# Linear attention moved between the delta-rule scan and softmax attention, with projections as its filler, and new bank and load rules

## The chip, the cores and the metric

One core of one Trainium2 chip runs the kernel. The metric is the device time in microseconds of one execution. The kernel before ran three times: 2265.18, 2269.78 and 2278.88 us, median 2269.78 us.

## The reference

Two layers of a diffusion backbone over 512 latent tokens `x` and 256 context tokens, model width 1024, float32. One layer, cut to what matters here:

```python
p = split(rmsnorm_and_modulate(h) @ w_in)          # one input projection, all head groups
# 1. multi-head latent attention (MLA), 8 heads
q, k, v = rmsnorm(cq) @ w_uq, rmsnorm(ckv) @ w_ukv  # ranks 384 and 256; rope on 32 columns
mla = softmax(q @ k.T * scale) @ v                  # latents see context + latents
# 2. gated delta rule (GDN), 4 heads, two directions, chunks of 64
v_new = u - w @ S
o = qd @ S + A @ v_new
S = S * g_last + k_end.T @ v_new                    # one step per chunk, strictly in order
# 3. gated linear attention (GLA), 4 heads, two directions
o = q_t S_t ; S_t = diag(exp(la_t)) S_(t-1) + k_t.T v_t
# all three: head norm, gate with silu(z), then one output projection
h = h + gate * rmsnorm(concat(mla, gdn, gla) @ w_out)
h = h + gate * rmsnorm(conv_ffn(...))
```

The last layer gives latents only, so its context queries, and the delta rule's outputs on context chunks, are left out.

## The kernel before, in words

All activations are held transposed, features on partitions and 768 tokens (context 0 to 255, latents 256 to 767) along the free axis. A projection by float32 weights is made of three products of split halves: `wsplit` (L196) loads a raw tile `wr` (three buffers), ACT casts its high half `wh` (L191) and DVE subtracts the low half `wl` (L192); `fprod` and its generator form `fsteps` then issue high*low, low*high and high*high matmuls over the column segments (512 latents, 256 context) into `bb`, a pair of PSUM banks (two such pairs). The other four banks have the names a, b, c and d; `ab(tags)` hands them out in turn, from the string it is given or from `self.tags`.

The order within one layer (`layer`, L311):

1. `project_in` computes the parts of the input projection that the delta rule needs, with `gdn_prep` and `gdn_tile` (products of 32x32 blocks for the inverse of each chunk pair, six tiles of two chunks) beside it. What the delta rule does not need is a generator `rest`: `gla_kq`, `gla_v`, `mla_in` and, last, `gate(1)`, the silu gates of the linear attention. At its end `project_in` runs the scan with `rest` as `self.fill`; `pace(n)` takes n steps of the generator, one step being a few matmuls.
2. `gdn_scan` (L969): 12 steps, both directions in one instruction stream, state `Sb`. A step multiplies state by key and query (16 matmuls of 128 columns, `ks`), makes `r = v - ks*eg` (L996, L997), multiplies by the inverse (`vp`, 16 matmuls), scales it (`vs`, L1008), multiplies by the keys (`up`, 16 matmuls) and adds it to the state (L1022, after POOL has multiplied the state by its decay, L1018). The output (`tq`, L1026, product with `AT`, L1041) and `head_out` (L1065: square, reduce, reciprocal root, POOL multiply L1075, two transposes, gate L1082) stand in the same step. `pace(8)` is called twice in a step. All its PSUM tiles rotate over b and c; the filler has a and d.
3. `mla_project` (L1250): products with `w_uk`, `w_uq`, `w_uv`; results that attention needs go to DRAM (`Kd`, `Qd`) and come back.
4. `attention` for the first pair of heads (`EP`, 1 of 4), then `gla`, then attention for the other three pairs with banks a and b. Per head and tile of 128 queries: scores into `bb`, row maximum (L1377), exponential into `P` (L1380), transposes of `P` (L215) copied out by ACT (L1394) or DVE (L1392), products with `V` into `a` or `b`.
5. `w_out` (k order 4, 5, 6, 7, 0, 1, 2, 3: delta rule and linear attention first), `post`, `prenorm`, feed-forward network.

The program text is not the final order. A list scheduler places each instruction on its engine by readiness in its own time model, with program order as the priority, so instructions of a later stage run ahead where their data and buffers allow it: attention is placed beside scan and linear attention alike. Pools bound this: a pool that takes the place of a closed one waits for the last reader of the old one. All DMAs are issued by SP, in one queue that keeps its order: a store that waits for its data (`ungates`, L1064) holds every load placed behind it.

Of the kernel before, what the change touches and what calls it, by code (L numbers as in the profile page):

```python
# [11 lines left out]
F32 = mybir.dt.float32  # L12
# [29 lines left out]
SN = (8, 8)  # L42
# [3 lines left out]
EP = (1, 1)  # L46
WO = ((4, 5, 6, 7, 0, 1, 2, 3), (4, 5, 6, 7, 0, 1, 2, 3))
SPF = 0
# [3 lines left out]
HB = 14  # L52
# [83 lines left out]
class Net:  # L136
# [40 lines left out]
    def s1(self, pool=None):  # L177
        return (pool or self.B).tile([128, 256], F32, name=self.nm("s"), tag="s", bufs=4 if pool is None else 6)
# [17 lines left out]

    def wsplit(self, src, n=1024):

        raw = self.raw()
        self.nc.sync.dma_start(raw[:, :n], src)  # L200
        his, los = [], []
        for o in range(0, n, 512):
            w = min(512, n - o)
            hi = self.W.tile([128, 512], F32R, name=self.nm("wh"), tag="wh", bufs=WB)
            lo = self.W.tile([128, 512], F32R, name=self.nm("wl"), tag="wl", bufs=WB)
            self.split(raw[:, o:o + w], hi[:, :w], lo[:, :w], self.nc.gpsimd if (o // 512, self.ph) in WP else None)
            his.append(hi)
            los.append(lo)
        return his, los
# [101 lines left out]
    def layer(self, l, later):  # L311
# [25 lines left out]
        Ap, self.A = self.pool("A")  # L337
        A0p, self.A0 = self.pool("A0")
        A1p, A1 = self.pool("A1")
        with self.ahead(HM):  # L340
            self.mla_project(A1)
# [7 lines left out]
        self.close(Bp)  # L349
        self.Xp, X = self.pool("X", "right")  # L350
# [10 lines left out]
        self.tags = "ab"  # L361
# [104 lines left out]
    def ada(self, l, mods, raw=None):  # L466
# [4 lines left out]
        for m in mods:  # L471
            for h in range(4):
                raws = []
                for k in range(2):
                    rt = (raw or self.raw)()
                    nc.sync.dma_start(rt, self.a["w_ada"][l, 4 * m + h, k])
# [76 lines left out]
    def project_in(self, later):  # L553
# [62 lines left out]
        def gdn(m):  # L616
            dst = dsts[m]
            for i in range(2):
# [3 lines left out]
                for a, b in segs:  # L622
# [7 lines left out]
                    if m != 1:  # L630
                        sq = self.F2.tile([128, 512], F32, name=self.nm("sq"), tag="sq", bufs=2)
# [7 lines left out]
        self.cq, self.ckv = [], []  # L639
        self.rr = self.small(12, "rr", 2)  # L640
# [48 lines left out]
        def projections():  # L689
# [29 lines left out]
        self.fill = [rest]  # L719
        self.tags = "ad"  # L720
        self.gdn_scan()
        self.fill = []
        drain(rest)
# [246 lines left out]
    def gdn_scan(self):  # L970
# [9 lines left out]

        for n in range(12):
# [24 lines left out]
            self.pace(SN[1])  # L1006
            vs = s1()
            nc.vector.tensor_tensor(vs.rearrange(h4, h=4), vp[:, :256].rearrange(h4, h=4),  # L1008
                                    self.eks[:, n].unsqueeze(2).to_broadcast(b4), op=ALU.mult)
            for d in range(2):  # L1010
                t, hf = ch[d] // 2, ch[d] % 2
                up = self.ab("bc")
# [10 lines left out]
            if need_o:  # L1023
                m = (3 if n < 4 else 15) - n
                vn, tq = s1(), s1()
                nc.vector.tensor_tensor(tq.rearrange(h4, h=4), ks[:, 256:].rearrange(h4, h=4), eg, op=ALU.mult)  # L1026
                if m < n:
                    nc.gpsimd.tensor_tensor(tq, tq, ost[m], op=ALU.add)
                nc.scalar.copy(vn, vp[:, :256])
                op = self.ab("bc")  # L1030
                for h in range(4):
                    for d in range(2):
                        e = d * 4 + h
                        self.mm(op[half[d], h * 64:(h + 1) * 64], self.AT[ch[d] // 2][half[d], e * 64:(e + 1) * 64],
                                vn[half[d], h * 64:(h + 1) * 64], True, True)
                if m > n:
                    ost[n] = self.C.tile([128, 256], F32, name=self.nm("ost"), tag="ost", bufs=4)
                    nc.vector.tensor_tensor(ost[n], tq, op[:, :256], op=ALU.add)
                    continue

                nc.vector.tensor_tensor(tq, tq, op[:, :256], op=ALU.add)  # L1041
                if n % 2 == 0:
                    lo = min(n, m) - 1
                    pieces = [(lo * 64, lo * 64 + 256)] if n < 10 else [(256, 384), (640, 768)]
                    zt = self.gates(0, pieces)
                first = (4 if n >= 10 else lo) if n % 2 == 0 else first
# [20 lines left out]
    def head_out(self, o, zt, cols, i):  # L1067
# [8 lines left out]
        ps = self.ab("cd" if i else "bc")  # L1076
# [8 lines left out]
    def gla(self):  # L1085
# [11 lines left out]
        for a, b in (CS, XS):  # L1097
# [34 lines left out]
            for d in range(2):  # L1132
# [22 lines left out]
                for st in steps:  # L1155
# [21 lines left out]
            def two():  # L1177
                t = self.B.tile([128, 1024], F32, name=self.nm("q2"), tag="q2", bufs=3)
                return t[:, :2 * n].rearrange("p (y c) -> p y c", y=2)
# [6 lines left out]
            for li, w in enumerate((32, 16, 8, 4, 2, 1, 0)):  # L1186
# [21 lines left out]
                for x in range(2):  # L1208
# [3 lines left out]
                    for i in range(nt):  # L1212
                        for c in range(2):
# [3 lines left out]
                                              ps[:, :nt * 128].rearrange("p (e j) -> p e j", j=64))  # L1217

            for i in range(nt):
                t, sl = t0 + i, slice(i * 128, (i + 1) * 128)  # L1220
                pieces = [(a + i // 2 * 256, a + i // 2 * 256 + 256)]
                if i % 2 == 0:
                    zt = self.gates(1, pieces)
# [22 lines left out]
                self.head_out(o, zt, [p0, p0 + 64], 1)  # L1246
                if i % 2:
# [3 lines left out]
    def mla_project(self, A1):  # L1251
# [12 lines left out]
        for lst, hi, lo, x in ((self.ckv, kvh, kvl, 0), (self.cq, cqh, cql, o)):  # L1264
            for d, h_, l_ in zip(lst, hi, lo):
                f = self.raw()
                nc.sync.dma_start(f[:, x:T], d[:, x:])
# [22 lines left out]
        for e in range(2):  # L1290
            rope = at("tab", 1)
            nc.sync.dma_start(rope, self.a["rope"][e])
            for p in range(4):
                wh, wl = self.wsplit(self.a["w_uq"][l, 2 * p + e], 384)
                ps = self.bb()
                self.fprod(ps, wh, wl, cqh, cql, self.osegs, 3)
# [10 lines left out]
        for t in range(6):  # L1307
# [8 lines left out]
            self.V.append(v)  # L1316

    def pair(self, pool, p):
# [8 lines left out]
        def raw(d, o):  # L1327
            f = self.raw()
            nc.sync.dma_start(f[:, o:T], d[:, o:])
# [236 lines left out]
```

## Time and profile before

| | |
|---|---|
| three timed runs | 2265.18 to 2278.88 us, median 2269.78 us |
| profiled execution | 2278.35 us |
| its span on the core | 2276.6 us |
| PE busy in the span | 2045.0 us, 90% |
| DVE, ACT, POOL busy | 1310.4, 1008.7, 536.0 us |
| mean granted TensorE clock | 0.934 of full speed |
| instructions | 44601 |

Time outside the span is 1.75 us, so a change of the span is a change of the time. The profiled execution lies 0.4% above the median. Columns of times are in microseconds, means in nanoseconds. A clock of 1.00 is 2.4 GHz and 0.50 is 1.2 GHz; values between are means over a stretch at both levels.

### The profile page before, as it was taken

To read this page: it belongs to the slowest core of one execution; us is meant where nothing else is said; L and a number is where in the kernel's file an instruction comes from. 1 tells how busy PE (TensorE), PEld (TensorE's weight loads), DVE (VectorE), ACT (ScalarE), POOL (GpSimd) and SP (SyncE) were. 2 spreads that over 40 slices of the span, in tenths; PEclk is the share of its full clock that TensorE was granted. 3 is DMA by queue.
4 is the path that set the end of the run, shared out by engine and by line. 5 is a ranking of instruction groups with operands and counts; after the bars stand their busy time and mean duration, and the time that the engine had idled before them with its cause. 6 is when DMAs were issued, how large, how long until landed. Compare 5 with 4: busy or idle time off the path is not lost. (4 is left out here: it accounts for less than half of the span.)

```text
span 2276.6 us, 44601 instructions
## 1 busy us (share of the span) xinstructions
PE 2045.0 (90%) x18168; PEld 1672.8 (73%) x18168; DVE 1310.4 (58%) x2474; ACT 1008.7 (44%) x1928; POOL 536.0 (24%) x897
## 2 busy tenths in 40 slices
PE   7898999888888799999999969988988777999996
PEld 4677777765667578888888857876766567888886
DVE  3354535668845743354454686556667757655556
ACT  4553323565464633332232456633446446543333
POOL 1342121135502310000010143413122613211102
PEclk8799999998898999999999979999989988999997
DMA  6232345422042354422212333111412053323322
GB/s 262 67 118 100 109 148 164 143 66 68 13 149 92 121 179 167 157 103 65 66 57 66 102 109 124 61 44 62 155 43 96 6 171 102 111 94 96 99 94 92
DMA packets 85134, 235.64 MB, mean 104 GB/s; under 512 B 9088, under 2 KB 24896, under 8 KB 84928
## 3 DMA queue, kind: packets, MB, share of 16 engines
q1 hardware_dynamic: 84928, 232.78, 30.7%
q8 instruction: 143, 2.34, 0.4%
q14 instruction: 63, 0.52, 0.1%
HBM read 204.04 MB, written 28.70 MB: 102 GB/s over the span
## 5 line engine op out<-in xcount | busy, mean ns | idle before, releaser
L212 PE MATMUL bb<-hh,wl 128*128 128x512 f32 (+1 forms) x1520 | 548.3, 361 | 18.0 <-DVE wl L192 10.9
L212 PE MATMUL bb<-hl,wh 128*128 128x512 f32 (+1 forms) x1520 | 542.0, 357 | 5.8 <-POOL hl L550 4.4
L192 DVE TENSOR_TENSOR wl<-wr,wh 128x512 fp32r<-128x512 f32 (+2 forms) x452 | 338.3, 751 | 362.3 <-ACT wh L191 361.0
L212 PE MATMUL bb<-hh,wh 128*128 128x512 f32 (+1 forms) x1520 | 540.2, 355 | 0.0
L191 ACT CAST wh<-wr 128x512 fp32r<-128x512 f32 (+2 forms) x452 | 274.1, 611 | 518.0 <-PE bb L212 370.3
L212 PEld LDWEIGHTS bb<-hh,wl 128*128 128x128 f32 x1520 | 293.2, 193 | 75.2 <-DVE wl L192 14.0
L212 PEld LDWEIGHTS bb<-hl,wh 128*128 128x128 f32 x1520 | 292.8, 193 | 49.4 <-POOL hl L550 7.8
L212 PEld LDWEIGHTS bb<-hh,wh 128*128 128x128 f32 x1520 | 292.9, 193 | 39.6 <-issue 2.1
L212 PE MATMUL bb<-g,wh 128*128 128x512 f32 (+1 forms) x1024 | 263.7, 349 | 2.3 <-DVE g L192 2.3
L1441 POOL TENSOR_SCALAR y<-u,fmt 128x512 f32<-128x512 f32 (+2 forms) x88 | 80.6, 917 | 527.1 <-ACT u L824 525.6
L212 PEld LDWEIGHTS bb<-g,wh 128*128 128x128 f32 x1024 | 181.5, 195 | 27.5 <-DVE g L192 3.3
L212 PE MATMUL bb<-g,wl 128*128 128x512 f32 (+1 forms) x512 | 180.3, 354 | 21.4 <-DVE wl L192 8.5
L212 PEld LDWEIGHTS bb<-g,wl 128*128 128x128 f32 x512 | 99.2, 195 | 36.9 <-ACT g L191 9.3
L824 ACT ACTIVATE u<-bb,fmt 128x512 f32<-128x512 f32 (+1 forms) x118 | 69.0, 613 | 85.0 <-PE bb L212 85.0
L212 PE MATMUL bb<-mh,wl 128*128 128x256 f32 (+1 forms) x256 | 85.2, 333 | 23.4 <-DVE wl L192 15.5
L1468 DVE TENSOR_TENSOR y<-y,bb 128x512 f32<-128x512 f32 (+2 forms) x80 | 54.8, 686 | 82.3 <-PE bb L212 82.2
L505 POOL TENSOR_TENSOR acc<-acc,sq 128x256 f32<-128x256 f32 (+1 forms) x48 | 49.5, 1031 | 183.9 <-ACT sq L503 180.9
L1442 DVE SCALAR_TENSOR_TENSOR y<-u,fmt,y 128x512 f32<-128x512 f32 (+2 forms) x88 | 72.3, 822 | 29.6 <-POOL y L1441 29.6
L212 PE MATMUL bb<-ml,wh 128*128 128x256 f32 (+1 forms) x256 | 84.1, 329 | 0.3
L1380 ACT ACTIVATE P<-bb,ast,srq 128x768 f32<-128x768 f32 (+1 forms) x80 | 72.6, 908 | 23.4 <-DVE ast L1378 14.5
L212 PE MATMUL bb<-mh,wh 128*128 128x256 f32 (+1 forms) x256 | 82.9, 324 | 0.0
L1377 DVE TENSOR_REDUCE ast<-bb 128x1 f32<-128x768 f32 (+1 forms) x80 | 67.2, 842 | 15.9 <-PE bb L212 15.6
(519 smaller groups left out, 3680.4 us busy)
## 6 DMA issues: line engine op xcount, KB each, us to landing
wr<-in_ffn_w_in SPq DMA_DIRECT2D x92, 512.0 KB, 3.5
wr<-in_w_ada SPq DMA_DIRECT2D x80, 512.0 KB, 3.9
wr<-in_ffn_w_out SPq DMA_DIRECT2D x48, 512.0 KB, 3.5
wr<-in_w_in SPq DMA_DIRECT2D x40, 512.0 KB, 4.3
wr<-in_w_out SPq DMA_DIRECT2D x32, 512.0 KB, 3.5
aw<-in_w_ada SPq DMA_DIRECT2D x16, 512.0 KB, 8.5
x<-in_xT SPq DMA_DIRECT2D x16, 384.0 KB, 8.7
wr<-in_w_uq SPq DMA_DIRECT2D x16, 192.0 KB, 2.6
```

What stands on the lines that cost most here:

```text
L191: self.nc.scalar.copy(hi, src)
L192: (eng or self.nc.vector).tensor_tensor(lo, src, hi.bitcast(F32), op=ALU.subtract)
L212: self.nc.tensor.matmul(out, l, r, start=start, stop=stop)
L505: (nc.vector, nc.gpsimd)[k % 2].tensor_tensor(acc[k % 2], acc[k % 2], sq, op=ALU.add)
L824: nc.scalar.activation(u[:, a + o:b + o], ps[:, off + a:off + b], AF.Identity, bias=bias)
L1377: nc.vector.reduce_max(st[:, 0:1], sc, axis=AX)
L1380: nc.scalar.activation(P[:, :w], sc, AF.Exp, bias=st[:, 0:1], scale=self.srq[:, t:t + 1], accum_out=st[:, 1:2])
L1441: nc.gpsimd.tensor_scalar(yv, u[:, lo + 1:lo + 1 + n], cw[1], self.fm(P_FCB + i), op0=ALU.mult, op1=ALU.add)
L1442: nc.vector.scalar_tensor_tensor(yv, u[:, lo:lo + n], cw[0], yv, op0=ALU.mult, op1=ALU.add)
L1468: nc.vector.tensor_tensor(y, y, p, op=ALU.add)
```

## The change

- Scan out of `project_in`: `project_in` returns `rest`, and the scan runs after it. The scan's pool C is now opened after F0 is closed; `sq` of the preparation moves from pool F2 to G.
- `gdn_scan` rewritten: fixed banks (`ks` and first half of `up` in b, `vp` and second half in c, both output products in d, `head_out` in a); the output products follow the state update; `head_out` and the store (`ungates`) of a step are put behind the next step's state update (`late`); `pace(5)` once per step.
- `gate(1)` moves ahead of `mla_in` in `rest`.
- `gla` runs between scan and attention, with a generator `beside` as filler: the remainder of `rest`, then `mla_project` (now a generator). `until` waits for the parts that `gla` needs; `pace` is called with `GN`.
- Attention follows: two pairs of heads before the mixed tiles are loaded, two behind; the last attention has banks a to d in place of a and b.
- `load`: the loads of weights and of `mla_project`'s and attention's operands are issued under a scheduler priority of 600 places.
- Buffers: `h` 14 to 12, `q2` 3 to 2, the scan's `s` 6 to 8.

```diff
-SN = (8, 8)
+SN = 5
-EP = (1, 1)
+EP = (2, 2)
+GN = (8, 6, 5)
+LP = 600
-HB = 14
+HB = 12
...
+    def load(self, out, src):
+
+        with self.tc.high_priority(offset=LP):
+            self.nc.sync.dma_start(out, src)
+
     def wsplit(self, src, n=1024):
 
         raw = self.raw()
-        self.nc.sync.dma_start(raw[:, :n], src)
+        self.load(raw[:, :n], src)
...
+    def until(self, what):
+
+        while what not in self.have:
+            self.pace(1)
...
+        F1p, F1 = self.pool("F1", "right")
         Fp, self.F = self.pool("F", "right")
+
+        F0p, self.F1 = self.pool("F0", "right")
+        rest = self.project_in(later)
+        self.close(F0p)
+        self.F1 = F1
         Cp, self.C = self.pool("C", "right")
-        F1p, self.F1 = self.pool("F1", "right")
-        F2p, self.F2 = self.pool("F2", "right")
-        self.project_in(later)
-        for p in (self.Hp, F2p, F1p, Cp, Fp):
+        self.fill = [rest]
+        self.gdn_scan()
+        for p in (Cp, Fp):
             self.close(p)
+
         Bp, self.B = self.pool("B", "right")
...
+        def beside():
+            yield from rest
...
+            yield from self.mla_project(self.A1)
+
+        self.tags = "ab"
+        self.fill = [beside()]
+        self.until("gla")
+        self.gla()
+        for g in self.fill:
+            drain(g)
...
-        with self.ahead(HA):
-            self.attention(A2, range(EP[l]))
-        with self.ahead(HG):
-            self.gla()
+        self.attention(A2, range(EP[l]))
...
-        self.tags = "ab"
+        self.tags = "abcd"
         self.attention(A2, range(EP[l], 4), mh, ml, mixed)
...
             yield from gla_v()
+            self.have.add("gla")
+            yield from gate(1)
+            self.have.add("gate")
             yield from mla_in(0)
             if not last:
                 yield from mla_in(1)
-            yield from gate(1)
...
-            ks = self.ab("bc")
-            for y in range(2 if need_o else 1):
-                for d in range(2):
-                    c = ch[d]
-                    for x in range(2):
-                        self.mm(ks[half[d], y * 256 + x * 128:y * 256 + x * 128 + 128],
-                                self.KQ[c // 2][:, x, y, half[d]], Sb[:, d, x], True, True)
+            ks = self.ab("b")
+            op = self.ab("d") if need_o else None
+            for y, z in ((0, ks), (1, op)):
+                if z is None:
+                    continue
+                for x in range(2):
+                    for d in range(2):
+                        self.mm(z[half[d], y * 256 + x * 128:y * 256 + x * 128 + 128],
+                                self.KQ[ch[d] // 2][:, x, y, half[d]], Sb[:, d, x], True, True)
...
-            self.pace(SN[0])
-            vp = self.ab("bc")
+            vp = self.ab("c")
...
-                up = self.ab("bc")
+                up = self.ab("bc"[d])
...
+            for go in late:
+                go()
+            late = []
+            self.pace(SN)
...
-                self.head_out(tq, zt, [64 * pos[(hf - n) % 2] for hf in range(2)], 0)
-                if n % 2:
-                    self.ungates(zt, 0, pieces)
+                late.append(output(n, tq, zt, [64 * pos[(hf - n) % 2] for hf in range(2)], n % 2))
...
+                self.pace(GN[0] * nt // 4)
...
-            self.fprod(ps, wh, wl, kvh, kvl, XC, 2)
+            yield from self.fsteps(ps, wh, wl, kvh, kvl, XC, 2)
```

Three places in the order of the instructions. First SP's queue in layer 0. `wr<-in_w_ada` and `wr<-in_w_in` are loads of weights, `zd<-zg` and `cg<-cg` stores of projections, `zt<-zd` loads of gates for the delta rule, and `md<-zt` is the store of the scan's first finished output. Before:

```order
L677 DMA cg_526_3924<-cg_3920 128x768
L476 DMA wr_4193<-in_w_ada 128x1024
L476 DMA wr_4195<-in_w_ada 128x1024
L677 DMA cg_550_4065<-cg_4061 128x768
L200 DMA wr_4215<-in_w_in 128x1024
L1064 DMA md_111_435<-zt_3687 256x1x256
L1057 DMA zt_4566<-zd_109_433 128x2x128 x2
L1267 DMA wr_4680<-cg_448_3467 128x768
L1267 DMA wr_4684<-cg_472_3607 128x768
L1267 DMA wr_4688<-cg_500_3771 128x768
```

After:

```order
L695 DMA gvd_456<-gvt_3407 768x1x128
L1099 DMA zt_3509<-zd_109_433 128x2x256
L1099 DMA zt_4034<-zd_109_433 128x2x256
L602 DMA zd_110_434<-zg_4004 128x768
L1106 DMA md_111_435<-zt_3509 256x1x256
L1099 DMA zt_4205<-zd_109_433 128x2x128 x2
L202 DMA wr_3988<-in_w_ada 128x1024
L202 DMA wr_4008<-in_w_in 128x1024
L202 DMA wr_4280<-in_w_ada 128x1024
L202 DMA wr_4282<-in_w_ada 128x1024
```

In both a store `md<-zt` stands ahead of loads; after, the weights that `rest` takes next (`wr<-in_w_ada`, `wr<-in_w_in`) stand behind the first store of the scan, where before they stood ahead of it.

Second, DVE in one scan step of layer 0. `s<-b,egs` at the first line number of each step is `r`, `s<-c,eks` is `vs`, `Sb` the state, `zt<-...` the gate of `head_out`, `hss` its sum of squares. Before, from one product with the state to its update:

```order
L996 TENSOR_TENSOR s_4448<-b_4439,egs_590 128x256
L192 TENSOR_TENSOR wl_5085<-wr_5078,wh_5084 128x512
L1298 TENSOR_TENSOR f_5046<-bb_5027,tab_4932 128x768
L997 TENSOR_TENSOR s_4448<-s_4449,s_4448 128x256
L1377 TENSOR_REDUCE ast_5154<-bb_5147 128x1
L1082 TENSOR_TENSOR zt_4425<-c_4434,zt_4425 128x2x64 x2
L1378 SCALAR_TENSOR_TENSOR ast_5154<-ast_5154,srq_4700 128x1
L1377 TENSOR_REDUCE ast_5180<-bb_5173 128x1
L1008 TENSOR_TENSOR s_4463<-c_4454,eks_591 128x256
L1026 TENSOR_TENSOR s_4482<-b_4439,egs_590 128x256
L1378 SCALAR_TENSOR_TENSOR ast_5180<-ast_5180,srq_4700 128x1
L1022 TENSOR_TENSOR Sb_3247<-Sb_3247,b_4465 64x2x64 x2
```

After, one whole step:

```order
L1036 TENSOR_TENSOR s_3605<-b_3595,egs_587 128x256
L256 RECIPROCAL hss_471_3569<-hss_471_3569 128x4
L1037 TENSOR_TENSOR s_3605<-s_3606,s_3605 128x256
L1046 TENSOR_TENSOR s_3620<-c_3611,eks_588 128x256
L1124 TENSOR_TENSOR zt_3509<-a_3575,zt_3509 128x2x64 x2
L1063 TENSOR_TENSOR Sb_3248<-Sb_3248,b_3625 64x2x64 x2
L1063 TENSOR_TENSOR Sb_3248<-Sb_3248,c_3633 64x2x64 x2
L1071 TENSOR_TENSOR s_3623<-d_3596,egs_587 128x256
L1114 TENSOR_REDUCE hss_485_3653<-s_3652 128x4
L1074 TENSOR_TENSOR ost_3650<-s_3623,d_3596 128x256
```

Before, attention (`ast`) and a projection's split (`wl`, `f`) stand between the parts of the step; after, the step stands alone, and the gate of the step before (`zt`) lies behind `vs`, ahead of the state update.

Third, PE in layer 1 where the output projection `bb<-mh,wl` begins. `c<-h,h`, `c<-gv,A` and `d<-cst,s` are linear attention. Before:

```order
L212 MATMUL c_18330<-gv_17817,A_18047 64x64 x8
L215 MATMUL d_18316<-cst,s_18306 128x128 x2
L212 MATMUL c_18364<-h_18358,h_18037 64x256 x2
L212 MATMUL c_18364<-h_18361,h_18040 64x256 x2
L212 MATMUL c_18364<-gv_17817,A_18047 64x64 x8
L215 MATMUL d_18353<-cst,s_18343 128x128 x2
L215 MATMUL d_18387<-cst,s_18377 128x128 x2
L212 MATMUL bb_19416<-mh_18404,wl_19413 128x256
L212 MATMUL bb_19416<-ml_18412,wh_19412 128x256
```

After, `c<-PT,V` and `b<-cst,P` are attention:

```order
L219 MATMUL bb_19416<-mh_18711,wh_19408 128x256
L219 MATMUL bb_19416<-mh_18712,wl_19409 128x256
L219 MATMUL bb_19416<-ml_18720,wh_19408 128x256
L219 MATMUL bb_19416<-mh_18712,wh_19408 128x256
L219 MATMUL c_19190<-PT_19179,V_17805 64x128
L219 MATMUL c_19190<-PT_19153,V_17814 64x128
L222 MATMUL b_19186<-cst,P_19174 128x128 x2
L219 MATMUL c_19190<-PT_19179,V_17814 64x128
L219 MATMUL c_19190<-PT_19153,V_17853 64x128
```

Before, the output projection follows the last of the linear attention, attention being done; after, attention ends last, and 50 matmuls of the output projection stand between its instructions.

## Rows read from the trace of the kernel before

**Rows 1.** The page, part 1: busy time and share of the span.
```profile
PE 2045.0 (90%) x18168; PEld 1672.8 (73%) x18168; DVE 1310.4 (58%) x2474; ACT 1008.7 (44%) x1928; POOL 536.0 (24%) x897
```

**Rows 2.** Windows cut at stage edges: window, length, busy time of each engine, granted clock, DMA.
```profile
113.00:285.00 172.00, 164.68 (x3239) 131.11 (x3238) 87.81 (x211) 70.58 (x144) 45.93 (x55) 0.98 0.33 110
...
490.00:640.00 150.00, 126.56 (x1350) 94.54 (x1351) 114.83 (x284) 84.08 (x177) 75.67 (x103) 0.86 0.14 48
640.00:660.00 20.00, 15.01 (x99) 10.33 (x95) 9.61 (x27) 11.38 (x28) 2.39 (x6) 0.74 0.56 202
...
1582.00:1626.00 44.00, 38.27 (x259) 29.72 (x260) 29.97 (x57) 14.90 (x29) 7.36 (x10) 0.92 0.61 193
...
1723.00:1831.00 108.00, 84.70 (x1032) 63.56 (x1028) 79.55 (x182) 51.31 (x109) 48.94 (x65) 0.95 0.14 47
1831.00:1850.00 19.00, 12.94 (x73) 11.57 (x74) 9.01 (x16) 9.57 (x21) 0.00 (x0) 0.67 0.80 277
2052.00:2109.00 57.00, 57.00 (x252) 47.03 (x251) 33.29 (x48) 21.14 (x36) 7.11 (x22) 1.00 0.29 93
```

**Rows 3.** Timeline, first matmul of the output projection in layers 0 and 1.
```profile
653.23 0.80 PE L212 MATMUL bb<-mh,wl 128*128 128x512 f32 x1 [0.72 <-ACT mh L191]
...
1836.39 0.58 PE L212 MATMUL bb<-mh,wl 128*128 128x256 f32 x1 [6.48 <-ACT mh L191]
```

**Rows 4.** Waits of SP's queue over the span: us, times, longest.
```profile
SPq L1064 <- DVE hss L1072: 52.0, 1, 52.0
```

**Rows 5.** Timeline of two scan steps of layer 1, without attention beside them.
```profile
1689.87 1.09 PE L212 MATMUL b<-Sb,kq 128*64 128x128 f32 x16
...
1691.31 0.39 DVE L996 TENSOR_TENSOR s<-b,egs 128x256 f32<-128x256 f32 x1
...
1698.53 2.03 PE L212 MATMUL b<-Sb,kq 128*64 128x128 f32 x16 [0.58 <-DVE s L1041]
...
1700.60 0.42 DVE L996 TENSOR_TENSOR s<-b,egs 128x256 f32<-128x256 f32 x1 [0.36 <-PE b L212]
...
1701.06 0.47 DVE L997 TENSOR_TENSOR s<-s,s 128x256 f32<-128x256 f32 x1
...
1703.41 1.12 PE L212 MATMUL c<-s,tt 64*64 64x64 f32 x16 [0.67 <-DVE zt L1082]
1704.57 0.42 DVE L1008 TENSOR_TENSOR s<-c,eks 128x256 f32<-128x256 f32 x1 [1.30 <-PE c L212]
...
1705.38 0.37 PE L212 MATMUL b<-s,ktok 64*64 64x64 f32 x2 [0.85 <-DVE s L1026]
...
1706.19 0.58 DVE L1022 TENSOR_TENSOR Sb<-Sb,b 64x128 f32<-64x128 f32 x2 [0.86 <-POOL s L1028]
```

**Rows 6.** Waits of PE in layer 1, 1535 to 1850 us.
```profile
PE d L215 <- POOL s L1075: 4.8, 4, 2.5
```

**Rows 7.** Windows of those two scan steps.
```profile
1690.00:1700.00 10.00, 5.86 (x82) 4.88 (x81) 4.90 (x14) 2.91 (x9) 2.66 (x4) 0.68 0.08 26
1700.00:1710.00 10.00, 5.08 (x59) 3.37 (x56) 4.63 (x14) 1.73 (x4) 2.66 (x4) 0.50 0.01 2
```

**Rows 8.** Line 997, all 24: ns min/median/max, first and last start.
```profile
L997 DVE TENSOR_TENSOR s<-s,s x24: 409/476/882, 256.7 to 1701.1; 128x256 f32<-128x256 f32 x24
```

**Rows 9.** Groups by line and shape in layer 1, 1535 to 1850 us: busy, mean ns.
```profile
L1377 DVE TENSOR_REDUCE ast<-bb 128x1 f32<-128x768 f32 x32 | 30.3, 948 | 6.7 <-PE bb L212 6.5
...
L1380 ACT ACTIVATE P<-bb,ast,srq 128x768 f32<-128x768 f32 x32 | 31.8, 994 | 10.0 <-DVE ast L1378 8.2 <-PE b L215 1.5
```

**Rows 10.** Timeline of one head's work on PE, in layer 1's attention.
```profile
1661.61 1.53 PE L212 MATMUL a<-PT,V 128*64 128x128 f32 x24
...
1666.08 0.60 PE L215 MATMUL d<-cst,P 128*128 128x128 f32 x4
```

**Rows 11.** Timeline of the start: last arrival of the latents and of the modulation weights.
```profile
24.32 0.63 ACT L503 ACTIVATE sq<-x 128x512 f32<-128x512 f32 x1 [2.94 <-DMA x<-in_xT]
...
41.70 1.08 PE L212 MATMUL d<-aw,cTs 128*32 128x256 f32 x8 [0.61 <-DMA aw<-in_w_ada]
```

More of the change, by code (lines that the diff above doesn't have):

```diff
@@ L177, in s1 @@
     def s1(self, pool=None):
-        return (pool or self.B).tile([128, 256], F32, name=self.nm("s"), tag="s", bufs=4 if pool is None else 6)
+        return (pool or self.B).tile([128, 256], F32, name=self.nm("s"), tag="s", bufs=4 if pool is None else 8)
     def bb(self):
@@ L328, in layer @@
         self.krope = self.dram([128, T], "krope")
+        F1p, F1 = self.pool("F1", "right")
         Fp, self.F = self.pool("F", "right")
+        F0p, self.F1 = self.pool("F0", "right")
+        rest = self.project_in(later)
+        self.close(F0p)
+        self.F1 = F1
         Cp, self.C = self.pool("C", "right")
-        F1p, self.F1 = self.pool("F1", "right")
-        F2p, self.F2 = self.pool("F2", "right")
-        self.project_in(later)
-        for p in (self.Hp, F2p, F1p, Cp, Fp):
+        self.fill = [rest]
+        self.gdn_scan()
+        for p in (Cp, Fp):
             self.close(p)
         Bp, self.B = self.pool("B", "right")
[L337 to L341, printed above, removed]
+        pools = []
+        def beside():
+            yield from rest
+            self.close(self.Hp)
+            for n in ("A", "A0", "A1"):
+                p, q = self.pool(n)
+                setattr(self, n, q)
+                pools.append(p)
+            yield from self.mla_project(self.A1)
[5 more added lines that the diff above has]
+            drain(g)
+        self.fill = []
+        Ap, A0p, A1p = pools
         self.close(A1p)
         A2p, A2 = self.pool("A2")
-        with self.ahead(HA):
-            self.attention(A2, range(EP[l]))
-        with self.ahead(HG):
-            self.gla()
+        self.attention(A2, range(EP[l]))
         self.close(Bp)
+        self.close(F1p)
         self.Xp, X = self.pool("X", "right")
@@ L475, in ada @@
                     rt = (raw or self.raw)()
-                    nc.sync.dma_start(rt, self.a["w_ada"][l, 4 * m + h, k])
+                    self.load(rt, self.a["w_ada"][l, 4 * m + h, k])
                     raws.append(rt)
@@ L630, in gdn @@
                     if m != 1:
-                        sq = self.F2.tile([128, 512], F32, name=self.nm("sq"), tag="sq", bufs=2)
+                        sq = self.G.tile([128, 512], F32, name=self.nm("sq"), tag="sq", bufs=2)
                         sqv = sq[:, :nt * 128]
@@ L639, in project_in @@
         self.cq, self.ckv = [], []
+        self.have = set()
         self.rr = self.small(12, "rr", 2)
@@ L718, in project_in @@
             drain(g)
[L719 to L723, printed above, removed]
+        return rest
     def gdn_gates(self):
@@ L979, in s1, with output, go @@
             return self.s1(self.C)
+        late = []
+        def output(n, tq, zt, cols, last):
+            def go():
+                self.head_out(tq, zt[0], cols, 0)
+                if last:
+                    self.ungates(*zt)
+            return go
         for n in range(12):
@@ L1038, in gdn_scan @@
                     nc.vector.tensor_tensor(ost[n], tq, op[:, :256], op=ALU.add)
-                    continue
-                nc.vector.tensor_tensor(tq, tq, op[:, :256], op=ALU.add)
+                else:
+                    nc.vector.tensor_tensor(tq, tq, op[:, :256], op=ALU.add)
+                    nc.gpsimd.tensor_tensor(tq, tq, ost[m], op=ALU.add)
+            for go in late:
+                go()
+            late = []
+            self.pace(SN)
+            if need_o and m < n:
                 if n % 2 == 0:
@@ L1044, in gdn_scan @@
                     pieces = [(lo * 64, lo * 64 + 256)] if n < 10 else [(256, 384), (640, 768)]
-                    zt = self.gates(0, pieces)
-                first = (4 if n >= 10 else lo) if n % 2 == 0 else first
+                    zt = (self.gates(0, pieces), 0, pieces)
+                    first = 4 if n >= 10 else lo
                 pos = [c - first if c - first < 4 else c - first - 4 for c in (n, m)]
-                self.head_out(tq, zt, [64 * pos[(hf - n) % 2] for hf in range(2)], 0)
-                if n % 2:
-                    self.ungates(zt, 0, pieces)
+                late.append(output(n, tq, zt, [64 * pos[(hf - n) % 2] for hf in range(2)], n % 2))
+        for go in late:
+            go()
     def gates(self, i, pieces):
@@ L1075, in head_out @@
         nc.gpsimd.tensor_tensor(ov, ov, ss.unsqueeze(2).to_broadcast([128, 4, 64]), op=ALU.mult)
-        ps = self.ab("cd" if i else "bc")
+        ps = self.ab("cd" if i else "a")
         for x in range(2):
@@ L1222, in gla @@
                 if i % 2 == 0:
+                    self.until("gate")
                     zt = self.gates(1, pieces)
@@ L1266, in mla_project @@
                 f = self.raw()
-                nc.sync.dma_start(f[:, x:T], d[:, x:])
+                self.load(f[:, x:T], d[:, x:])
                 self.split(f[:, x:T], h_[:, x:], l_[:, x:])
@@ L1295, in mla_project @@
                 ps = self.bb()
-                self.fprod(ps, wh, wl, cqh, cql, self.osegs, 3)
+                yield from self.fsteps(ps, wh, wl, cqh, cql, self.osegs, 3)
                 f = at("f", 2)
@@ L1328, in raw @@
             f = self.raw()
-            nc.sync.dma_start(f[:, o:T], d[:, o:])
+            self.load(f[:, o:T], d[:, o:])
             return f
```

16 lines of the change are left out of this document (8 added, 8 removed).

## The prediction

> **What bounds the kernel now.** I read the page first: PE is busy for 90% of the span [rows 1], so the change can win only where PE idles or runs at the lower clock. Windows cut at stage edges show where that is [rows 2]. The preparation of layer 0 (113 to 285 us) has PE busy for 164.68 of 172 us at 0.98 of the clock; a stretch of the feed-forward network (2052 to 2109) has no gap at all. The gaps lie in the stages that the change touches: 126.56 of 150 us in linear attention of layer 0 (490 to 640), 15.01 of 20 at clock 0.74 where its output projection starts (640 to 660), 84.70 of 108 in linear attention of layer 1 (1723 to 1831), and 12.94 of 19 at 0.67 just behind it. So I compare the time from the end of the preparation to the first output-projection matmul, 285 to 653.23 us in layer 0 and 1582 to 1836.39 in layer 1 [rows 2, 3]. What lies ahead and behind keeps its instructions.
>
> Two waits stand out in layer 1. The output projection's first matmul sat 6.48 us behind ACT's split of a mixed tile [rows 3], and one store of a scan output held SP's queue for 52.0 us [rows 4].
>
> Last, the scan. Where attention no longer lies beside it, its step is a chain: from the product of state and query at 1689.87 to the next at 1698.53, and on DVE from 1691.31 to 1700.60, so 8.7 and 9.3 us [rows 5].
>
> **Start.** The latents land at 24.32 us, the last of the early modulation weights at 41.70 [rows 11]. The new priority puts those weights' loads ahead in SP's queue; nearly the same bytes are ahead of the last of them. I take 0, with 3 us to either side.
>
> **Preparation, layer 0.** A matmul of 512 columns takes 57.00/252 = 0.226 us [rows 2], one of 256 I estimate at half of that, so 0.17 for the mean of the two. `gate(1)` adds 96 of them (+16); 52 of `mla_in` (-9) and 40 small ones of the scan (-4, at some 0.1 us) leave. That is +4 to 289. The scan's pool now waits for the last reader of the preparation's: between 0 and 8 us, I take 4. The scan starts at 293.
>
> **Scan step.** The new order takes the output off the state's chain and puts each product in a bank of its own, and in six of layer 0's twelve steps, and about 8.5 of layer 1's, nothing else stands beside it. What remains from state to state, at the lower clock: half of the 2.03 us product (1.0), L996 0.42, L997 0.6, inverse 1.12, L1008 0.42, key product 0.81 (1705.38 to 1706.19), L1022 twice 0.58 with a gap (1.19), and about 0.5 for four hand-overs: 6.0 us [rows 5]. The low end is 4.9, with PE's parts at full clock (1.09 for the 2.03, the others scaled alike); the high end is the 9.3 measured before.
>
> The clock is the term to watch. The windows of the two steps have 0.68 and 0.50 [rows 7], the same 16 matmuls taking 1.09 us at 1689.87 and 2.03 at 1698.53 [rows 5]. The Trainium skill, page "TensorE: Matmul & The Clock Gate", section "What's actually happening", says that the throttled state is the default and activity lifts it. The trace agrees in these two windows; the rule speaks against a scan with nothing beside it. By it a step takes 6.0; by the full clock 4.9, and the sum would be 20.5 x 1.1 = 22 us lower.
>
> L997 takes 409 to 882 ns, 476 in the median [rows 8]; my 0.6 lies between. The Trainium skill, page "GPSIMD Engine Reference", section "1. Specifications", says that POOL shares its memory interfaces with VectorE, which collides with DVE instructions that have two operands in SBUF; L997 is one. The spread of the rows fits that, but they don't show what ran beside the slow ones. By the slowest row each step would be 0.3 longer, the sum 6 us higher.
>
> Layer 0: 12 x 6.0 = 72. Filler enters only about three steps, 102 matmuls of `mla_in` or 17 us of PE; what the idle of those steps doesn't take I put at 10 (between 0 and 17). The order shows why the others are bare: the weights for the filler stand behind the first scan output's store in SP's queue. So 82 us, to 375.
>
> **Linear attention, layer 0.** Before, 59% of attention's 736 matmuls stood between its first and last instructions; now attention comes after it, 31% already there by readiness. In their place come `mla_project` (234 x 0.18 = 42 us) and 150 matmuls of `mla_in` (25.5); 28% of 101 us of attention leaves (-28), and 3 us of modulation comes: +42. The 101 us is an estimate: 32 head tiles at 768 keys at 2.7 us each (1.53 for a `V` product, 0.60 for four transposes, the rest scores [rows 10]) and 16 short ones at a third. If its own chain through DVE (114.83 us busy) sets the length, the stretch stays at 150; if PE's work adds in full, it is 192. I take the middle, 171: to 546.
>
> **Attention, layer 0.** 69% remains, 70 us of PE. Beside nothing, it runs on what the ends have shown: 15.01/20 busy [rows 2] makes 93 us, PE alone 70. DVE's row maximum (0.948 us) and ACT's exponential (0.994) [rows 9] lie under the 2.7 us per head tile, and four banks instead of two let transposes run ahead of `V`; I take 82. It ends at 628, where before the output projection began at 653.2 and then lost about 3 us at clock 0.74. Layer 0: -28 us.
>
> **Layer 1.** The scan starts at 1582 - 3 + 4 = 1583. Its first 3.5 steps run beside 138 matmuls of `mla_project`, 40 us (before, 44 for the like stretch, 38.27 of it PE [rows 2]; without filler, 21). Then 8.5 steps x 6.0 = 51, and 3 to start linear attention: 1677. This takes between the 108 us of before and 123 (10 us more of attention, 5 of 24 `w_uv` matmuls); 116, to 1793. Of attention's 86 us of PE (32 head tiles) 40% is left, 34, and 50 matmuls of the output projection (6 us) lie in it: between 40 and 40/0.75 = 53, I take 47, to 1840. Before, the projection began at 1836.4 with 4.5 us lost at clock 0.67 and the 6.48 us wait; those 50 matmuls (5.7 us) are already done in mine: 1840 against 1846.6. Layer 1: -6.6 us.
>
> **Buffers.** `h` with 12 for 14 and `q2` with 2 for 3 I cost at nothing: linear attention's chain is held by DVE's work, under which one buffer less is hidden. If that cover is gone, the most they can cost is the idle share of PE there, 23 us in each layer [rows 2]; I keep that for the upper end.
>
> **Sum.** 2278.35 - 28 - 6.6 = 2243.7 us for an execution like the profiled one, which lies 0.4% above the median: 2243.7 x 2269.78/2278.35 = 2235. By the measure used here, 1% either way (2247 and 2292) is about what can be told from no change.
>
> **Rivals.**
> 1. *Linear attention's chain sets its length.* DVE was busy for 114.83 of 150 us and 79.55 of 108 [rows 2], with attention on it; with attention gone the filler's matmuls could all fall into its gaps. Against it: the splits of the filler's weights come back on DVE. Stretches stay at 150 and 108: 21 + 8 us less, 2206.
> 2. *The stretches go to their upper ends.* The filler adds in full, attention alone waits as at 640 to 660: +21, +7, +11, +6, 45 us, giving 2280: no change. For it: both engines that attention needs now do nothing but attention, one head at a time. Against: four banks.
> 3. *The scan's step doesn't shorten, and the kernel is slower.* Place: the bare steps. `head_out` of the last step still stands on DVE ahead of the state update (`zt`, behind `vs`), and PE waited for its POOL multiply (L1075) four times for 4.8 us in layer 1 [rows 6]; an in-order engine that waits there holds the state's chain behind it. Price: 9.3 - 6.0 = 3.3 us x 20.5 steps = 68, so 2303. It decides from a step of 7.7 us on, where the gain is gone.
> 4. *Loads don't run ahead.* The order shows scan stores still ahead of weights; the priority does not part them. This is already in my sum (six bare steps); with filler in all, layer 0 would gain 10 to 15 us more in the linear-attention stretch, inside rival 1.
>
> **Chances.** Forecast 0.44, its own range 2215 to 2257; rival 1 0.22, rival 2 0.20, rival 3 0.14. Below 2247 fall about 0.33 of the forecast's and all of rival 1's: 0.55. Above 2292 is rival 3: 0.14. The rest, 0.31, is within 1%. The range goes from below rival 1 (2185) to between rivals 2 and 3 (2295).
>
> **What would show it.** Right: a scan step of 5.5 to 6.5 us with a clock near 0.5 in layer 0's first six steps; the first output-projection matmul of layer 0 near 628 us, of layer 1 near 1840 less layer 0's gain; PE in linear attention busier than 126.56/150. Wrong: steps over 7.7 us; a linear-attention stretch over 192 us; attention of layer 0 over 93 us; a weight load that waits behind the store for longer than one step; or a difference outside 285 to 660 and 1580 to 1850 us of more than 5 us.

## The result, and the profile after

The changed kernel takes 2299.39 us in the median (four runs, 2294.58 to 2307.69) against 2274.33 for the kernel before (four runs): ratio 1.0107, 95% interval 1.0079 to 1.0134. It is slower by 1%, where 2235 was forecast.

The page's first part, after, answers to [rows 1]:

```profile
PE 2048.3 (89%) x18168; PEld 1682.4 (73%) x18168; DVE 1317.0 (57%) x2474; ACT 1012.6 (44%) x1929; POOL 538.1 (23%) x897
```

PE does the same work (2048.3 against 2045.0 us) in a span that is 24.5 us longer. The matmuls of the output projection say where it went: one group of 128 in each layer, with first and last start behind the durations (min/median/max in ns). Before, layer 0 and layer 1:

```profile
L212 PE MATMUL bb<-mh,wl x128: 276/388/796, 653.2 to 745.8; 128*128 128x512 f32 x64, 128*128 128x256 f32 x64
...
L212 PE MATMUL bb<-mh,wl x128: 276/279/582, 1836.4 to 1898.0; 128*128 128x256 f32 x128
```

After:

```profile
L219 PE MATMUL bb<-mh,wl x128: 276/388/579, 666.9 to 754.2; 128*128 128x512 f32 x64, 128*128 128x256 f32 x64
...
L219 PE MATMUL bb<-mh,wl x128: 276/279/420, 1853.3 to 1923.5; 128*128 128x256 f32 x128
```

The last of them is 754.2 - 745.8 = 8.4 us late in layer 0 and 1923.5 - 1898.0 = 25.5 in layer 1, so layer 1 adds 17.1. What lies between the two stretches and behind the second differs by 1 us each.

Windows after, cut at the stages (columns as in [rows 2]): scan, linear attention and attention alone in layer 0, then scan beside the projections, bare scan, linear attention, attention alone (two pieces) in layer 1.

```profile
291.00:388.00 97.00, 75.21 (x949) 54.70 (x949) 49.75 (x147) 24.45 (x60) 24.79 (x39) 0.89 0.22 73
388.00:579.00 191.00, 165.19 (x1436) 131.97 (x1437) 140.39 (x286) 98.64 (x175) 78.53 (x98) 0.88 0.38 126
579.00:680.00 101.00, 93.41 (x756) 72.08 (x755) 57.44 (x155) 60.62 (x139) 12.43 (x32) 0.97 0.27 96
1587.00:1625.00 38.00, 34.36 (x234) 26.70 (x234) 24.22 (x47) 14.70 (x30) 8.88 (x13) 0.81 0.61 192
1625.00:1693.00 68.00, 52.05 (x634) 39.21 (x625) 42.76 (x114) 18.04 (x42) 17.05 (x27) 0.87 0.18 57
1693.00:1823.00 130.00, 95.69 (x1008) 74.88 (x1008) 95.39 (x205) 70.60 (x133) 53.33 (x67) 0.84 0.19 61
1823.00:1850.00 27.00, 25.90 (x226) 20.77 (x223) 16.97 (x42) 19.99 (x39) 2.94 (x8) 0.94 0.47 160
1850.00:1870.00 20.00, 18.68 (x180) 15.36 (x178) 9.07 (x24) 9.85 (x22) 1.91 (x4) 1.00 0.19 62
```

The scans are nearly as short as forecast (89 and 98 us from first to last instruction, where they were spread over 224 and 152). The linear-attention stretches grew, to 191 and 130 us from 150 and 108 [rows 2], the second at clock 0.84 where it was 0.95. PE's idle time in layer 0's did not shrink: 25.8 us, before 23.4. Where attention stands alone PE has few gaps: it is busy for 93.41 of 101 and for 25.90 of 27 and 18.68 of 20 us.

The bare scan step, from one `r` (L1036) to the next in the timeline of layer 1:

```profile
1652.66 0.42 DVE L1036 TENSOR_TENSOR s<-b,egs 128x256 f32<-128x256 f32 x1
...
1653.66 0.68 PE L219 MATMUL c<-s,tt 64*64 64x64 f32 x16
1654.39 0.42 DVE L1046 TENSOR_TENSOR s<-c,eks 128x256 f32<-128x256 f32 x1 [0.78 <-PE c L219]
...
1654.87 0.45 PE L219 MATMUL b<-s,ktok 64*64 64x64 f32 x8 [0.53 <-DVE s L1046]
...
1657.46 0.42 DVE L1036 TENSOR_TENSOR s<-b,egs 128x256 f32<-128x256 f32 x1
```

It takes 4.8 us; the bare steps of both layers take 4.8 to 6.0. The 16 matmuls with the inverse take 0.68, not the 1.12 of [rows 5]: the granted clock is 0.95 between 1652 and 1672 us.

SP's queue in layer 0's scan, timeline and waits:

```profile
290.03 0.79 SPq L602 DMA_DIRECT2D zd<-zg  x1
318.02 0.56 SPq L1106 DMA_DIRECT2D md<-zt  x1
322.52 1.17 SPq L1099 DMA_DIRECT2D zt<-zd  x2
323.80 0.54 SPq L202 DMA_DIRECT2D wr<-in_w_ada  x1
...
SPq L1106 <- DVE zt L1124: 26.2, 1, 26.2
```

The store of the first scan output holds the queue for 26.2 us, and the first weight load for the filler follows at 323.80. Six steps were bare, then two with all the filler that the scan got took 20.8 and 14.2 us (from the starts of L1036), and the rest were bare again.

### The profile page after: what moved, and what is told of

Its sections match the earlier page's. It is cut to its first block, busy times and chain, and to the rows that moved or that the text cites. A ratio compares the mean times of both kernels' runs of the same rounds, so it can differ in the third digit from the quotient of the medians.

```text
span 2301.1 us, 44646 instructions
## 1 busy us (share of the span) xinstructions
PE 2048.3 (89%) x18168; PEld 1682.4 (73%) x18168; DVE 1317.0 (57%) x2474; ACT 1012.6 (44%) x1929; POOL 538.1 (23%) x897
```

## The experiments

All ratios are to the kernel before, run beside them; the brackets are 95% intervals.

**First: which part costs?** Theory A blames linear attention's new place, theory B the scan that is left without filler, theory C the loads. e1 puts linear attention back behind the first attention; e2 puts only the scan's edit on the kernel before.

```diff
 e1, changed kernel
-        self.fill = [beside()]
-        self.until("gla")
-        self.gla()
+        for _ in beside():
+            pass
...
         self.attention(A2, range(EP[l]))
+        self.gla()
 e2, kernel before: gdn_scan, its pools and SN = 5 as changed, first attention
     in banks a and b (before: a and d); all else as before
 e3, changed kernel
-        with self.tc.high_priority(offset=LP):
-            self.nc.sync.dma_start(out, src)
+        self.nc.sync.dma_start(out, src)
 e4, changed kernel
-SN = 5
+SN = 16
```

> The changed kernel, with linear attention put back behind the first attention and with no filler of its own (projections and the latent-attention projections run out between the scan and it). Theory A (linear attention became longer because other stages' work stands in its in-order engines: 200 and 138 us from the scan's end to its last output, where 171 and 119 were forecast): gives back 15 us or more, under 2285 us. Theory B (the scan alone is the loss, since its PE idles without filler): no more than 5 us either way, 2294 to 2304. Theory C (loads): the same as B.

> The kernel before with the scan's edit alone: run after the preparation, banks fixed, output late, one pace of 5; the order of projections, attention, linear attention, their banks, buffers and loads as before. Theory A: faster than before or the same, 2255 to 2275, as the bare step of 5.2 us leaves linear attention as it was. Theory B: slower than before by 15 us or more, over 2289, as the work that lay in the scan's gaps now follows it.

> The changed kernel with loads issued without priority. Theory C (the priority moves loads to where they collide with others or wait in front of stores that are needed): gives back 10 us or more, under 2289. Theories A and B: within 5 us of 2299, or slower since some loads come later.

> The changed kernel with 16 filler steps per scan step in place of 5. Theory B: gives back 10 us or more, under 2289, as projections fill the scan again. Theory A: also faster, but only by what leaves the linear attention's stretch, 5 to 10 us. If weights held behind the scan's first store are what keeps the filler out, no change (within 5 us of 2299).

e1: 1.0109 [1.0064, 1.0154]. e2: 1.012 [1.009, 1.015]. e3: 1.0098 [1.0076, 1.012]. e4: 1.0048 [1.0028, 1.0067]. Theories A and C fall: neither linear attention's old place nor loads without priority give anything back that is clear of noise. The scan's edit alone costs in total what the whole change costs, and more filler in the scan gives back half, as theory B had it. Between 293 and 446 us e4's window has PE busy for 141.62 of 153, where the scan of the changed kernel had 75.21 of 97:

```profile
293.00:446.00 153.00, 141.62 (x1338) 112.14 (x1335) 86.81 (x197) 45.10 (x94) 32.52 (x43) 0.94 0.44 150
```

**Second: what in the scan's edit?** e5 moves only the scan's pool behind the preparation; e6 and e7 put only the new body into the old place, with 5 and 16 filler steps. e8 takes loads' priority and four banks without the rest.

```diff
 e5, kernel before
+        F0p, self.F1 = self.pool("F0", "right")
+        rest = self.project_in(later)
+        self.close(F0p)
         Cp, self.C = self.pool("C", "right")
...
         self.tags = "ad"
         self.gdn_scan()
 e6 (e7 with 16), kernel before: gdn_scan as changed
-        self.tags = "ad"
         self.gdn_scan()
 e8, kernel before: load() as changed, and
-        self.tags = "ab"
+        self.tags = "abcd"
         self.attention(A2, range(EP[l], 4), mh, ml, mixed)
```

> The kernel before with the scan only moved behind the preparation (its pool in the place of the closed ones), its body, banks and two paces of 8 as before. If the place is the cost (theory B2: the scan can no longer start under the preparation's last products): slower by 10 us or more, over 2284. If the scan's body or its filler is the cost (B1, B3): within 5 us of 2274.

> The kernel before with only the scan's new body, in the old place, one pace of 5 per step. Theories B1 (too little filler per step) and B3 (the body): slower by 15 us or more, over 2289. Theory B2: within 5 us of 2274 or faster.

> The same with one pace of 16 per step, as many filler steps as the two paces of 8 before. Theory B1: 10 us or more faster than the run with 5, near or under 2274. Theory B3 (the body's order or its banks, which leave the filler only bank a): still over 2284.

> The kernel before with only the loads' priority and the four banks in the last attention; scan and linear attention untouched. From the run without priority (2 us below the changed kernel) I expect no effect of the loads; with the banks 0 to 5 us faster: 2269 to 2275.

e5: 1.0062 [1.0038, 1.0086]. e6: 1.0345 [1.0313, 1.0376]. e7: 1.0241 [1.0218, 1.0264]. e8: 1.032 [1.0299, 1.0341], far off what I expected. The place costs half. e6 and e7 tell less than they were meant to: without the `tags` line the first attention, too, has bank a alone, a handicap that e13 below puts at some 50 us on the changed kernel; the step from 5 to 16 still gives 1.0%.

e8's windows show the hold: layer 0's and layer 1's linear attention without attention beside it, and between them the attention that follows in layer 0.

```profile
506.00:603.00 97.00, 55.09 (x628) 40.27 (x623) 61.51 (x131) 25.61 (x48) 52.84 (x58) 0.56 0.06 19
603.00:697.00 94.00, 88.07 (x745) 69.24 (x746) 55.82 (x154) 60.88 (x139) 14.71 (x33) 0.96 0.31 103
1739.00:1831.00 92.00, 38.93 (x531) 29.62 (x532) 52.85 (x96) 20.41 (x41) 40.77 (x47) 0.55 0.12 36
...
L218 PE MATMUL c<-PT,V x152: 272/273/325, 603.6 to 1912.2; 128*64 128x128 f32 x152
```

Linear attention uses banks c and d; attention's first product into bank c comes at 603.6 us, when it is over. Until then PE has 55.09 of 97 us at clock 0.56.

**Third: undoing one of these on the changed kernel.**

```diff
 e9 (e12 with SN = 16 as well), changed kernel, layer 1 alone; there the rest
     of the projections also runs out ahead of linear attention
+            Cp, self.C = self.pool("C", "right")
             rest = self.project_in(later)
 e10, changed kernel
-        self.tags = "abcd"
+        self.tags = "ab"
 e11, kernel before: load() as changed, nothing else
```

> The changed kernel, with the scan's pool opened ahead of the preparation in layer 1 (as before), so that the scan needn't wait for the preparation's end there; all else, its body and one pace of 5 included, as changed. Theory P (layer 1's loss is the scan's late start, 15 us in the run with only the place changed): gives back 10 to 18 us, 2281 to 2289. Theory E (the early start gives no gain with the new body, as e6 lost 76 us in the old place): slower than 2299.

> The changed kernel with banks a and b, not a to d, in the last attention. Theory K (banks c and d keep attention from running beside linear attention, which holds c and d: e8's attention stood still from 506 to 603 us): gives back 5 to 20 us if part of the last attention can be taken ahead. If program order already holds it behind: within 3 us of 2299.

> The kernel before with only the loads' priority. If e8's 72 us are the banks: within 5 us of 2274. If they are the loads: over 2330.

> Pool of layer 1 as before and 16 filler steps per scan step, together on the changed kernel. If the two losses add: 2299 - 12 - 10 to 18 = 2269 to 2277, level with before. If they overlap: 2280 to 2290.

e9: 1.0116 [1.0092, 1.0139]. e10: 1.0135 [1.0115, 1.0156]. e11: 1.0005 [0.9988, 1.0022]. e12: 1.0104 [1.0084, 1.0124]. The loads do nothing that shows, so e8's loss is the banks; in the changed order, where the last attention follows linear attention anyway, they cost nothing. e9 and e12 miss: the place that costs when it is changed alone gives nothing when it alone is changed back. Nor does 16 gain there what it gained in e4.

**Fourth: what keeps attention out of the scan's steps?** In the traces 196 of layer 1's attention matmuls (products for scores and with `V`) start within the scan before, 12 after. e13 leaves bank a to attention (the last one in a and b), e14 takes two buffers `s` back, so that the scan's pool no longer overlaps attention's, e15 does both, e16 also sets `EP` to (1, 1).

```diff
 e13, e15, e16, changed kernel
-        self.tags = "ab"
+        self.tags = "a"
         self.fill = [beside()]
...
-        ps = self.ab("cd" if i else "a")
+        ps = self.ab("cd" if i else "c")
 e14, e15, e16
-        ... tag="s", bufs=4 if pool is None else 8)
+        ... tag="s", bufs=4 if pool is None else 6)
```

> The changed kernel with bank a left to attention during the scan (head_out in c, the projections for attention and its first pairs in a, the last pairs in a and b); eight buffers s stay, so the scan's pool still overlaps attention's. Theory Z (attention waits for bank and memory both): no gain, 2292 to 2310. If the bank alone keeps it out: under 2285, and attention's matmuls stand between the scan's steps.

> The changed kernel with six buffers s in the scan, so that its pool (from 147.8 KB) lies beside attention's (to 147.4 KB). Theory Z: no gain alone, 2292 to 2305. If memory alone keeps attention out: under 2285.

> Both edits together. Theory Z: attention stands in the scan's steps in layer 1 (some 200 of its matmuls, 12 before) and none behind linear attention; 15 to 35 us under the changed kernel, 2264 to 2284. If the scan's and linear attention's own order is the cost: over 2290 still.

> Both edits and one pair of heads ahead of the mixed tiles, as in the kernel before, which leaves 174 in place of 258 of layer 0's attention matmuls behind linear attention. Theory Z: 3 to 10 us under the run with both edits. Otherwise the same as it.

e13: 1.036 [1.034, 1.038]. e14: 1.0157 [1.0135, 1.0178]. e15: 1.0187 [1.0165, 1.0209]. e16: 1.0142 [1.0113, 1.0171]. The lock is as described: only e15 and e16 have attention in layer 1's scan (216 and 196 matmuls; 12 in e13 and e14), and e15 is 2353.64 - 2314.82 = 39 us under e13. But with bank a alone for its first pairs, and `head_out` in c, the kernel is some 50 us dearer (e13's 1.036 against e10's 1.0135), and in total letting attention in by these means doesn't pay. The two layers differ, though. The same group of output-projection matmuls in e15:

```profile
L219 PE MATMUL bb<-mh,wl x128: 276/388/797, 679.6 to 776.4; 128*128 128x512 f32 x64, 128*128 128x256 f32 x64
...
L219 PE MATMUL bb<-mh,wl x128: 276/279/583, 1871.8 to 1934.3; 128*128 128x256 f32 x128
```

Against the kernel before, layer 0 loses 30.6 us (8.4 in the changed kernel), but layer 1 adds only 5.7 (17.1): in this one execution letting attention in pays in layer 1, and layer 0 takes it back. That e14, which only takes two buffers away, is no faster than the changed kernel fits the theory; that it may be a little slower I can't explain.

e13 shows one thing more. Its pace is 5, as in the changed kernel, yet in layer 0 its first nine scan steps take 13.6 to 17.9 us with filler in them, and SP's queue has the filler's weights in time:

```profile
292.79 0.52 SPq L602 DMA_DIRECT2D zd<-zg  x1
293.41 1.10 SPq L202 DMA_DIRECT2D wr<-in_w_ada  x2
297.08 0.33 SPq L202 DMA_DIRECT2D wr<-in_w_in  x1
307.48 2.27 SPq L202 DMA_DIRECT2D wr<-in_w_ada  x2
```

So the six bare steps are not the held queue's doing by itself: with the banks dealt out differently the loads come ahead of the store.

**Last: pace against body, and layer against layer.** e17 is e2 with `SN = 16`; e18 is e5 in layer 0 only.

> The kernel before with the scan's edit (place and body) as in e2, but 16 filler steps per scan step. If the half of the loss that the place doesn't explain is the pace: 2285 to 2293, level with the run with the place alone (1.006). If it is the body: 2296 to 2305, as e2 (1.012).

> The kernel before with only the scan's place changed, and in layer 0 only. If the place costs in layer 1 (16 us from post to post in e5's trace) and gains in layer 0 (6 us): 2264 to 2271, ratio 0.996 to 0.999, below both kernels. If the place costs in both: 2280 or more.

e17: 1.005 [1.0031, 1.007], level with e5. e18: 0.9994 [0.9973, 1.0014]. So on the kernel before, in totals, the scan's edit costs 0.7% by its pace (e2 to e17), and with the old body its place costs 0.7% in layer 1 (e5 to e18). That e17 is level with e5 looks as if the body's new order cost and gained nothing, but the layers say otherwise. The output projection in e5, then in e17:

```profile
L212 PE MATMUL bb<-mh,wl x128: 278/394/794, 648.8 to 737.8; 128*128 128x512 f32 x64, 128*128 128x256 f32 x64
...
L212 PE MATMUL bb<-mh,wl x128: 276/280/583, 1845.2 to 1907.7; 128*128 128x256 f32 x128
...
L218 PE MATMUL bb<-mh,wl x128: 276/388/792, 655.2 to 752.0; 128*128 128x512 f32 x64, 128*128 128x256 f32 x64
...
L218 PE MATMUL bb<-mh,wl x128: 276/279/480, 1836.2 to 1905.1; 128*128 128x256 f32 x128
```

Against the kernel before (745.8 and 1898.0), e5 gains 8.0 us in layer 0 and loses 17.7 in layer 1; e17 loses 6.2 and 0.9. These are single executions, and e11, level with the kernel before in total, differs from it by 5.5 us in a layer; the 14 and 17 us between e5 and e17 are beyond that. No version was faster than the kernel before.

## Why the prediction was wrong

**Right.** The step shortened, so rival 3's mechanism is dead, though the time lies beside its 2303: bare steps took 4.8 to 6.0 us, most of them near the low end of 4.9 and not at the 6.0 of the sum. (With all three of PE's parts scaled, as the text says, that low end is 4.7.) Layer 0's scan ended at 378 us where 375 was worked out, which is in part luck: shorter bare steps and longer steps with filler made up for each other. Layer 1's ran 98 us where 91 was worked out, and its attention alone took 47 us, as forecast. The six bare steps came as the order showed. The start moved by 1 us.

**The step that failed** is "I take the middle, 171" (and 116 in layer 1): that half of the filler's work would fall into linear attention's gaps. It took 191 us, the full sum (192), and 10 more, which stood in no term, passed between the scan's end and its start. In layer 1 it was 130, over the upper end of 123, at a lower clock than before. Attention alone in layer 0 was mis-sized too: 82 us in the sum, 101 to its end, of which 46 matmuls of the output projection are some 8 (at the prediction's 0.17 each), so 93, the upper end. PE was busy for 85 us of these where 70 had been worked out; the 1.53 us of [rows 10] are the `V` products of two heads and not of one, so scores and transposes must cost more than was left for them. All this is rival 2's case, which I gave 0.20. Even its 2280 was short: by its terms layer 0 comes 4 us late and layer 1 another 6, and 8.4 and 17.1 were measured.

**What I left out** is a sum over the stage. These two windows before and two after, from the preparation's end to the end of attention and linear attention:

```profile
285.00:660.00 375.00, 327.45 (x3061) 254.13 (x3061) 236.25 (x569) 185.83 (x372) 118.39 (x165) 0.90 0.32 103
1582.00:1850.00 268.00, 216.40 (x2197) 167.87 (x2198) 181.75 (x417) 130.39 (x260) 76.34 (x111) 0.89 0.27 90
```

```profile
285.00:680.00 395.00, 338.66 (x3240) 262.71 (x3239) 250.00 (x593) 186.26 (x380) 118.06 (x170) 0.90 0.32 106
1582.00:1875.00 293.00, 233.30 (x2410) 183.18 (x2411) 191.66 (x439) 136.08 (x273) 84.39 (x118) 0.86 0.26 84
```

Before, PE was busy for 327.45 of 375 us, 87%. Work that the change moved out of or into the stretch nearly cancels (-16 for `gate(1)`, +13), so my 335 us, from 293 to 628, asked for about 95% (320.69 us of work up to 653.2, less 3). At the 78% that the scan's window shows after (75.21 of 97), 82 us of scan would leave, as an estimate, 254 us of work for the other 253: no gap at all in linear attention and attention. After, the share is 86% (338.66 of 395); in layer 1, 81% before and 80% after. The scan's time was not idle before: 224 us of it in layer 0 held projections, their next stage and attention. Emptied, it lets linear attention begin earlier, but the work that lay in it comes back behind it, nearly one for one: 38.6 us more of PE's work made layer 0's linear attention 41 us longer. Why the filler did not fall into its gaps no run shows.

So why slower, not the same? One half is shown: filler that stays outside the scan, 0.7% on the kernel before and 0.6% on the changed one (e4). The other half is open. With the old body it is a layer-1 scan that can no longer start under the preparation (0.7%). With the new body the place hardly costs there (e17 adds 0.9 us in layer 1), and undoing it on the changed kernel gave nothing (e9): the preparation ends 9 us later in its trace and the rest is 16 shorter, so the scan's early steps seem to delay the preparation that they run under. In e4's trace layer 0 is level with the kernel before (its last matmul of that group at 746.3, before 745.8), and the 10 us that are left lie in layer 1 (1908.8, before 1898.0), where attention still stands outside the scan; e15's layer 1 points the same way, but no run has it without e15's other cost.

**The clock.** I let the bare scan run at the lower level, 1.2 GHz, by [rows 7], and named a clock near 0.5 in layer 0's first six steps as a sign of being right. They ran at 0.94, mostly at the upper level, 2.4 GHz:

```profile
291.00:321.00 30.00, 24.26 (x400) 17.71 (x400) 20.54 (x62) 9.63 (x24) 10.35 (x17) 0.94 0.10 36
```

The window of layer 1's bare steps has 0.87 (1625 to 1693 us). That made the bare steps shorter than in the sum, and yet the kernel won nothing by it. What fell was linear attention's clock in layer 1, from 0.95, with PE busy for 84.70 of 108 us, to 0.84, with PE busy for 95.69 of 130. I had taken the level from steps of 9.3 us, in which PE was busy for half the time [rows 7], and put it on steps half as long. The Trainium skill's page "TensorE: Matmul & The Clock Gate", section "What's actually happening", has activity lift a throttled default. The 0.56 and 0.55 of e8's linear attention, with PE busy for 55.09 of 97 and 38.93 of 92 us, agree with it. By it alone I could not have said on which side the bare step would fall.

## What to carry to other kernels

Before you credit a shorter chain, add up what the busiest engine did beside it and ask what busy share your forecast needs of that engine in the whole stage; if it is higher than the trace shows in any stretch with that mix, doubt the gain. When a stage moves, list the resources that let its neighbours in (PSUM banks by name, the addresses of pools, the place in a DMA queue): banks and addresses together shut attention out of layer 1's scan here, and freeing one of them alone did not let it back in. Split a total by layer before you add effects up: e5 and e17 are level in total and far apart in each layer. And give the filler to the bare chain: 16 steps for 5 gained 0.6 to 1.0% in three of four pairs.

## What the runs showed that I had not expected

Linear attention by itself takes 92 us in layer 1, with the clock at 0.55 (e8); beside attention, 108 at 0.95 [rows 2]. Attention's first pairs with one PSUM bank instead of two, and `head_out` moved to another, cost some 50 us (e13 against e10), more than any stage's order did. Two banks more, where another stage holds them, cost 2345.81 - 2273.57 = 72 us (e8), and nothing where it doesn't (e10).
